# Gated-delta inverse: blocks of 16 solved on VectorE by way of DRAM, with small moves around it

## The chip, the cores and the metric

One core of one Trainium2 chip runs the whole program. The metric is the device time of one execution in microseconds (us); the kernel before was run three times, and its median is what a change is held against. The trace is of one more execution, taken by the profiler.

## The reference

The input is one sequence of 256 tokens, 1024 wide, in float32. Two "first" layers and then two "second" layers run over it. A first layer is a norm, a product with `w_in`, four mixers on the slices of its result, a product with `w_out`, a residual, and a gated feed-forward network (FFN). The four mixers are a (HGRN2) and b (gated linear attention), both chunkwise linear attention; c (latent attention with a softmax); and d, the gated delta rule. The second layers have other mixers and are not touched, but for a norm. What mixer d computes for each chunk of 64 tokens and each head is:

```
m   = strict_lower(kb @ kc^T * lmask)              # 64 x 64
sol = triangular_solve(m + eye, [v * b, kb * exp(b)])
u, w = split(sol)
v_new = u - w @ state
o     = (q * exp(b)) @ state + a_qk @ v_new
state = exp(b_last) * state + (k * exp(b_last - b))^T @ v_new
```

The linear mixers a and b need, for each chunk, the lower triangle of `attn[i, j] = sum_d q[i, d] k[j, d] exp(b[i, d] - b[j, d])`.

## The kernel before

The 256 tokens are two tiles t of 128 (all 128 partitions). Weights come from DRAM in units of up to 512 KB (`raw`, three buffers), whose DMAs SyncE (SP) issues in program order. Each is split into a rounded high part (`wh`, ScalarE, L300) and a remainder (`wl`, VectorE or GpSimd, L303), and each product is three passes on TensorE (L329 to L331, or L375 and L376). PSUM has eight banks in four pairs, acc, pc, pd and pa. Mixers a and b take their scratch from pa, c from pc, d from pd (`pt()`), and `acc()` hands out acc and pa in turn.

The mixers are Python generators that emit instructions in pieces; `PLAN1` and `RUN1` say whose piece comes next (d's preparation, b's projections, d's inverse and output, a's projections, b's attention, c, a's attention). From what was emitted a list scheduler fixes the order of instructions on each engine before the program runs. An engine works strictly in that order, so an instruction that waits holds up all that stand behind it on its engine. Between layers `steps()` and `sum_sq()` run the residual and the norms, and `warm()` may put in bf16 matmuls whose result nobody reads.

Mixer d prepares, per tile, `MT` and `AT` (L1128, L1129): the triangular matrix transposed, four heads of 128x128, each with two chunks of 64 on its diagonal. Then (I + M) is inverted by doubling blocks. At a level w = 2, 4, 8 or 16, with the inverse `V` of the diagonal blocks of w known and `T` its transposed even blocks, TensorE multiplies `MT` with `T` (L1176, four heads a tile), VectorE masks the product into `X` (L1177), TensorE multiplies `X` with `V` (L1191), VectorE adds that to `V` (L1192), TensorE transposes `V` (L1197) and ScalarE copies the transpose into `T` (L1199). GpSimd clears `X` (L1174). Before the first level VectorE writes the blocks of 2 with masks (L1154, L1155). Levels 32 and 64 go by smaller pieces (L1168, L1184). With the inverse in hand come d's output steps for tile 0, the state, and tile 1 (L1205 to L1240), each closed by a norm over heads (`head_norm`, L601 to L608), transposes of its result (L415), and the hi and lo part of it (L417, L418) for the product with `w_out`.

The linear mixers a and b (`gla`) build the triangle the same way on scaled queries and keys (`gl_r`, `gl_e`, L733, L727; products L743, L751): the diagonal block comes from PSUM by a multiplication with the identity (L705, VectorE), the levels 64 by a ScalarE copy (L756), and 32 down to 1 by copies under a mask (L760, VectorE). Then L768 and L769 multiply with the values. Mixer c's product with `w_in` is 48 passes of 128x416 (L329 to L331), alternately into acc and pa.

Of the kernel before, what the change touches and what calls it, by code (L numbers as in the profile page):

```python
# [11 lines left out]
F = mybir.dt.float32  # L12
# [34 lines left out]
WARM = ((0, 0, 0), (0, 2, 0))  # L47
# [92 lines left out]
class K:  # L140
    def __init__(self, ctx, tc, a):
        self.tc, self.nc, self.a = tc, tc.nc, a
        e = ctx.enter_context
        self.cst = e(tc.tile_pool(name="cst", bufs=1))
        self.wp = e(tc.tile_pool(name="wp", bufs=1))
        self.xp = e(tc.tile_pool(name="xp", bufs=1))
        self.zp = e(tc.tile_pool(name="zp", bufs=1))
        self.sm = e(tc.tile_pool(name="sm", bufs=4))
        self.ps = e(tc.tile_pool(name="ps", bufs=1, space=PSUM))
        self.units, self.made, self.nexti, self.emitted = [], {}, 0, 0  # L150
# [12 lines left out]
        nc.vector.memset(self.mhalf, -0.5)  # L163

    def masks(self):
# [5 lines left out]
        nc.gpsimd.tensor_copy(self.cu, t)  # L171

# [250 lines left out]
    def sum_sq(self, a, b, psum=False):  # L423
# [5 lines left out]
        self.warm(sc, WARM[self.g == "a"][0 if psum else 2])  # L429
# [261 lines left out]
    def gla(self, nft, b, qm, k, v, finish, g):  # L691
# [8 lines left out]
        for t in range(2):  # L700
# [4 lines left out]
            nc.vector.tensor_tensor(A[t], p, self.ident[:, None, :].to_broadcast([128, 4, 128]), OP.mult)  # L705
# [3 lines left out]
        for lv, s in enumerate((128, 64) + LEVELS):  # L709
# [181 lines left out]
    def mixer_c(self, l, xT):  # L891
# [12 lines left out]
        pz = self.tm(xT, (("c", l), 2, 416))  # L904
# [93 lines left out]
    def mixer_d(self, l, xT):  # L998
# [3 lines left out]
        code = [self.z([128, 16], "b_code", "b") for _ in range(2)]  # L1002
# [38 lines left out]
        def prep(t):  # L1041
# [5 lines left out]
            nbeta = self.s(4, "d_nbeta")  # L1047
            nc.vector.tensor_scalar(nbeta, beta, -1.0, None, op0=OP.mult)
# [42 lines left out]
            nc.vector.tensor_tensor(kb, qk[:, 4:8], bc4(nbeta, 64), OP.mult)  # L1091
# [9 lines left out]
            kT = self.z([128, 2, 2, 128], "d_kT")  # L1101
            nc.gpsimd.memset(kT, 0.0)
# [11 lines left out]
            for par in range(2):  # L1114
                rr = slice(par * 64, par * 64 + 64)
                nc.scalar.activation(kT[rr, par], p2[rr, :2], AF.Copy)
            if t:
                o["qeT"] = self.z([128, 2, 128], "d_qeT")
                nc.scalar.activation(o["qeT"], p2[:, 2:], AF.Copy)
# [22 lines left out]
        for t in range(2):  # L1142
            T[t] = self.z([128, 4, 64], "d_T")
            V[t] = self.z([128, 4, 128], "d_V")
            nc.gpsimd.tensor_copy(part(T[t], 2), half(mb(self.ident), 2, 0))
            nc.gpsimd.tensor_copy(V[t], mb(self.ident))
        for t in range(2):
            MT = st[t]["MT"]
# [3 lines left out]
            at = lambda i, n: self.cu[:, i * 64:i * 64 + 64].rearrange("p (b s) -> p b s", s=n)[:, None].to_broadcast(  # L1152
                [128, 4, 64 // n, n])
            nc.vector.copy_predicated(part(T[t], 2), at(6, 2), half(p, 2, 0))  # L1154
            nc.vector.copy_predicated(half(V[t], 1, 1), at(5, 1), half(MT, 1, 1))  # L1155
        for lv in range(6):
            w = 2 << lv
            X = [None] * 2
            for t in range(2):
# [17 lines left out]
                nc.vector.tensor_tensor(half(X[t], w, 0), part(p, w), half(mb(ms[:, lv * 128:lv * 128 + 128]), w, 0), OP.mult)  # L1177
            for t in range(2):
                p = self.pt()[:, :256].rearrange("p (h i) -> p h i", h=4)
                if w >= 32:  # L1180
# [11 lines left out]
                nc.vector.tensor_tensor(v, v, part(p, w), OP.add)  # L1192
# [37 lines left out]
        nc.scalar.activation(wT[:64], pw, AF.Copy)  # L1230
# [7 lines left out]
        for h in range(4):  # L1238
            nc.tensor.matmul(po[:, h], st[1]["qeT"][:, h // 2], Sp[:, h], start=True, stop=False)
# [548 lines left out]
```

## Time and profile before

| | before |
|---|---|
| times of three runs, us | 1532.23, 1531.16, 1528.4 |
| median, us | 1531.16 |
| profiled execution: its own time, its span, us | 1537.6, 1535.9 |
| mean granted TensorE clock | 0.989 of full |
| busy, share of the span | TensorE 96%, VectorE 69%, ScalarE 55%, GpSimd 18% |
| bytes moved, rate | 233.99 MB, 152 GB/s |

Read it so: the span is what the profiler saw from the first to the last instruction of the profiled execution. PE is TensorE's matmuls, PEld its weight loads (they run beside matmuls), DVE is VectorE, ACT ScalarE, POOL GpSimd, SP SyncE. The clock is the part of full speed that the chip granted to TensorE. In rows of the timeline the first number is when an instruction, or a group of neighbours of one kind, began, the second its busy time. Since matmuls are pipelined, the records of a group overlap the next: what a group costs TensorE is read from start to start.

### The profile page before, as it was taken

The numbers are of one execution on the slowest core, as the hardware profiler recorded it, in microseconds if no ns is written. First come the engines' busy times: TensorE is split into PE (matmuls) and PEld (weight loads), VectorE is DVE, ScalarE is ACT, GpSimd is POOL, SyncE is SP. The second block draws the span as 40 slices with busy tenths as digits, with TensorE's granted clock in tenths as the row PEclk, the third lists the DMA queues.
The fourth block names the chain that finished last, engine by engine and source line by source line (L and its number), as shares of the span: only waits on it lengthen the run. The fifth ranks groups of instructions, "written<-read, shape, count | busy, mean of one in ns | idle before, by whom it ended". The sixth has DMA issues, their size and how long they took to land.

```text
span 1535.9 us, 23550 instructions
## 1 busy us (share of the span) xinstructions
PE 1481.3 (96%) x8731; PEld 1287.0 (84%) x8739; DVE 1062.3 (69%) x1891; ACT 837.2 (55%) x1520; POOL 281.8 (18%) x375
## 2 busy tenths in 40 slices
PE   7999999999998999999999999999998999999998
PEld 7988888888897987888978887888877888888886
DVE  6897577667789756777766866566657695666655
ACT  5735456556574534655545665544554675544453
POOL 1544210000254322000042122000024231100010
PEclk9999999999999999999999999999999999999999
DMA  7422146666452214666646334566653533465663
GB/s 238 150 84 100 52 140 184 190 190 213 135 161 78 93 42 134 183 192 187 206 131 184 110 112 124 187 191 191 211 186 111 163 121 108 133 192 187 190 202 108
DMA packets 156418, 233.99 MB, mean 152 GB/s; under 512 B 11700, under 2 KB 118158, under 8 KB 156302
## 3 DMA queue, kind: packets, MB, share of 16 engines
q1 hardware_dynamic: 156302, 232.48, 49.0%
q8 instruction: 69, 1.13, 0.3%
q14 instruction: 47, 0.39, 0.1%
HBM read 231.40 MB, written 1.05 MB: 151 GB/s over the span
## 4 chain that ended last, share of the span: by engine, by line
PE 79%; DVE 10%; ACT 4%; POOL 2%; DMA 2%; issue 2%; SPq 0%; ACTq 0%; DVEq 0%; POOLq 0%
PE pa L375 8%; PE pd L375 7%; PE acc L329 7%; PE acc L331 7%; PE acc L330 7%; PE pc L329 5%; PE pc L331 5%; PE pc L330 5%; PE pd L376 4%; PE pa L376 4%; PE pa L329 2%; PE pa L331 2%; PE pa L330 2%; DVE wl L303 2%; DVE gl_r L733 1%
## 5 line engine op out<-in xcount | busy, mean ns | idle before, releaser
L303 DVE TENSOR_TENSOR wl<-raw,wh 128x1024 fp32r<-128x1024 f32 (+4 forms) x424 | 487.1, 1157 | 310.2 <-ACT wh L300 308.6
L300 ACT ACTIVATE wh<-raw 128x1024 fp32r<-128x1024 f32 (+4 forms) x420 | 433.1, 1035 | 368.9 <-PE pc L331 92.1
L303 POOL TENSOR_TENSOR wl<-raw,wh 128x1024 fp32r<-128x1024 f32 (+1 forms) x26 | 61.2, 2358 | 641.8 <-ACT wh L300 611.2
L375 PE MATMUL pa<-xT,wh 128*128 128x512 f32 x392 | 145.9, 397 | 0.0
L375 PE MATMUL pd<-xT,wh 128*128 128x512 f32 x392 | 145.7, 397 | 0.0
L376 PE MATMUL pd<-xT,wl 128*128 128x256 f32 x392 | 110.2, 281 | 0.3 <-DVE wl L303 0.3
L376 PE MATMUL pa<-xT,wl 128*128 128x256 f32 x392 | 110.1, 281 | 0.0
L375 PEld LDWEIGHTS pd<-xT,wh 128*128 128x128 f32 x392 | 73.6, 188 | 16.8
L375 PEld LDWEIGHTS pa<-xT,wh 128*128 128x128 f32 x392 | 73.7, 188 | 12.3
L330 PE MATMUL acc<-wl,f_h 128*128 128x512 f32 x200 | 78.0, 390 | 0.0
L330 PE MATMUL pc<-wl,f_h 128*128 128x512 f32 x200 | 77.8, 389 | 0.0
L331 PE MATMUL pc<-wh,f_l 128*128 128x512 f32 x200 | 77.5, 389 | 0.0
L331 PE MATMUL acc<-wh,f_l 128*128 128x512 f32 x200 | 77.3, 391 | 0.0
L376 PEld LDWEIGHTS pd<-xT,wl 128*128 128x128 f32 x392 | 74.0, 189 | 3.6 <-DVE wl L303 0.5
L376 PEld LDWEIGHTS pa<-xT,wl 128*128 128x128 f32 x392 | 74.1, 189 | 3.6
L330 PE MATMUL acc<-wl,xT 128*128 128x512 f32 (+4 forms) x200 | 71.1, 357 | 1.6 <-DVE wl L303 1.6
L329 PE MATMUL acc<-wh,xT 128*128 128x512 f32 (+4 forms) x200 | 71.5, 361 | 1.2 <-ACT xT L510 0.8
L329 PE MATMUL pc<-wh,f_h 128*128 128x512 f32 x200 | 71.4, 390 | 0.0
L331 PE MATMUL acc<-wh,xT 128*128 128x512 f32 (+4 forms) x200 | 70.4, 354 | 0.6 <-DVE xT L512 0.6
L329 PE MATMUL acc<-wh,f_h 128*128 128x512 f32 x200 | 67.0, 391 | 0.0
L329 PE MATMUL acc<-wh,mT 128*128 128x512 f32 (+2 forms) x136 | 51.4, 387 | 1.6 <-ACT mT L510 1.4
L330 PE MATMUL acc<-wl,mT 128*128 128x512 f32 (+2 forms) x136 | 51.3, 378 | 0.0
(651 smaller groups left out, 3852.5 us busy)
## 6 DMA issues: line engine op xcount, KB each, us to landing
raw<-in_w_in_dram SPq DMA_DIRECT2D x84, 512.0 KB, 4.2
raw<-in_w_mlp_up_dram SPq DMA_DIRECT2D x64, 512.0 KB, 3.7
raw<-in_w_mlp_down_dram SPq DMA_DIRECT2D x64, 512.0 KB, 3.6
raw<-in_ffn_w_gate_dram SPq DMA_DIRECT2D x44, 512.0 KB, 3.6
raw<-in_ffn_w_up_dram SPq DMA_DIRECT2D x44, 512.0 KB, 3.9
raw<-in_ffn_w_down_dram SPq DMA_DIRECT2D x44, 512.0 KB, 3.6
raw<-in_w_out_dram SPq DMA_DIRECT2D x32, 512.0 KB, 3.6
raw<-in_w_ple_gate_dram SPq DMA_DIRECT2D x16, 512.0 KB, 4.4
```

What stands on the lines that cost most here:

```text
L300: nc.scalar.activation(h[:, p], raw[:, p], AF.Copy)
L303: e.tensor_tensor(l[:, p], raw[:, p], h[:, p].bitcast(F), OP.subtract)
L329: t.matmul(out, ah, bh, start=first, stop=False, skip_group_check=True)
L330: t.matmul(out, ah, bl, start=False, stop=False, skip_group_check=True)
L331: t.matmul(out, al, bh, start=False, stop=last, skip_group_check=True)
L375: t.matmul(out[f], h[:, k, c], xT.both[:, :, kk], start=kk == 0, stop=False, skip_group_check=True)
L376: t.matmul(out[f][:, 1], l[:, k, c], xT[0][:, kk], start=False, stop=kk == 7, skip_group_check=True)
L733: nc.vector.tensor_tensor(R[:, j].rearrange("p h (b s) -> p h b s", s=s), ev[:, ft[j], :, 1][:, None].to_broadcast([128, 2, 128 // s, s]), ...
```

## The change

Mixer d's levels 2, 4 and 8 are gone, and so are the masks that fed them. In their place the program does this: both tiles of `MT` go to a DRAM buffer `scr`, whose pitch of 129 rows per head makes the blocks of 16 on the diagonal addressable by one stride; one DMA brings the 64 blocks of 16x16 back, one block to a partition (`Z`, 1024 pieces of 64 bytes); VectorE inverts all of them by forward substitution (seven pairs of a product and a reduction over up to 98 elements, then two pairs over 512); `Y` goes in pieces of 64 bytes to a second DRAM buffer `scv`, which was zeroed at the program's start; and two DMAs (256 KB each) bring the block-diagonal `V` of both tiles. TensorE transposes `V`, ScalarE copies it into `T`, and the old loop goes on from level 16. The sign of M is turned, so copies get `scale=-1` and one addition becomes a subtraction.

Around it: `gla` takes its diagonal by a ScalarE copy and a GpSimd `affine_select`, and level 32 by four small ScalarE copies for each tile in place of one masked copy; mixer c's product goes into the bank pair acc alone; `kT` in d's preparation is one dense copy, and its matmul reads 64 partitions; `code` lies in another pool; the constants shrink; and the norm before three of the layers gets four warm matmuls (128x512, bf16) for tile 0. At the start four more DMAs of 132 KB zero `scv`.

```diff
-WARM = ((0, 0, 0), (0, 2, 0))
+WARM = ((0, 0, 0, 4), (0, 2, 0, 0))
...
-        self.warm(sc, WARM[self.g == "a"][0 if psum else 2])
+        self.warm(sc, WARM[self.g == "a"][0 if psum else 2 + (self.near > 0 and self.kinds[self.near] in PEORD)])
...
+        zero = self.z([128, 258], "zero", "d")
+        nc.gpsimd.memset(zero, 0.0)
+        for i in range(4):
+            nc.sync.dma_start(self.at(self.scv, i * 128 * 258, [[258, 128], [1, 258]]), zero)
...
-            nc.vector.tensor_tensor(A[t], p, self.ident[:, None, :].to_broadcast([128, 4, 128]), OP.mult)
+            nc.scalar.activation(A[t], p, AF.Copy)
+            nc.gpsimd.affine_select(out=A[t], in_=A[t], pattern=[[0, 4], [1, 128]], compare_op=OP.is_ge, fill=0.0,
+                                    base=0, channel_multiplier=-1)
...
+                if s == 32:
+                    for r in (0, 64):
+                        nc.scalar.activation(A[t][r:r + 32, :, r + 32:r + 64], pv[r:r + 32, :, r // 2:r // 2 + 32], AF.Copy)
+                    continue
...
-        pz = self.tm(xT, (("c", l), 2, 416))
+        pz = self.tm(xT, (("c", l), 2, 416), outs=self.first_banks("acc"))
...
-            kT = self.z([128, 2, 2, 128], "d_kT")
-            nc.gpsimd.memset(kT, 0.0)
...
+            kT = self.z([128, 4, 128], "d_kT")
+            nc.scalar.activation(kT[:, :4 if t else 2], p2[:, :4 if t else 2], AF.Copy)
...
-                    nc.tensor.matmul(p[:, f], kT[:, par, f], qkT[:, f], start=True, stop=True)
+                    nc.tensor.matmul(p[:, f], kT[rr, f], qkT[rr, f], start=True, stop=True)
...
+        for t in range(2):
+            nc.sync.dma_start(dense(self.scr, t), st[t]["MT"])
+        Z, Y = self.z([64, 256], "d_Z"), self.z([64, 256], "d_Y")
+        nc.sync.dma_start(Z.rearrange("p (j r) -> p j r", r=16), blocks(self.scr))
+        nc.gpsimd.tensor_copy(Y, self.cb[:64, 512:768])
+        tmp, U = self.z([64, 512], "d_tmp"), self.z([64, 64], "d_U")
+        for r in range(1, 8):
+            p = tmp[:, :2 * r * r].rearrange("p (a c j) -> p a c j", a=2, c=r)
+            nc.vector.tensor_tensor(p, view(Z, r, [[136, 2], [0, r], [16, r]]), view(Y, 0, [[136, 2], [16, r], [1, r]]), OP.mult)
+            nc.vector.tensor_reduce(view(Y, r, [[136, 2], [16, r]]), p, AX.X, OP.add, negate=True)
...
+        nc.sync.dma_start(blocks(self.scv), Y.rearrange("p (c r) -> p c r", r=16))
...
+            nc.sync.dma_start(V[t], dense(self.scv, t))
             p = four()
             for h in range(4):
-                nc.tensor.transpose(p[:, h], MT[:, h], self.ident)
...
-            nc.vector.copy_predicated(part(T[t], 2), at(6, 2), half(p, 2, 0))
-            nc.vector.copy_predicated(half(V[t], 1, 1), at(5, 1), half(MT, 1, 1))
-        for lv in range(6):
+                nc.tensor.transpose(p[:, h], V[t][:, h], self.ident)
+            T[t] = self.z([128, 4, 64], "d_T")
+            nc.scalar.activation(part(T[t], 16), half(p, 16, 0), AF.Copy)
+        for lv in range(3, 6):
```

The line numbers of the kernel of the change are higher by 16 to 31 than those of the same code before: L329 to L331 are L345 to L347 there, L303 L319, L415 L431, L733 L752, L751 L770, L760 L783, L1176 L1207, L1240 L1271. The order of the instructions moves at three places. First TensorE in the first layer, before, where level 8 ends and mixer c's product (128x416) begins:

```order
L1176 MATMUL pd<-d_T,d_MT 128x64 x4
L1191 MATMUL pd<-d_V,d_X 128x64 x8
L1197 MATMUL pd<-cf,d_V 128x128 x8
L415 MATMUL pa<-cf,hn_o 128x128 x2
L329 MATMUL pa<-wh,xT 128x416
L330 MATMUL pa<-wl,xT 128x416
```

and in the kernel of the change the place where the inverse comes back to TensorE, behind the end of b's attention (L791, L792, L431) and ahead of a's (L720) and c's (L951):

```order
L792 MATMUL pa<-a_v,gl_a 128x64
L1184 MATMUL pd<-cf,d_V 128x128 x8
L1207 MATMUL pd<-d_T,d_MT 128x64 x8
L431 MATMUL pa<-cf,hn_o 128x128 x2
L720 MATMUL pa<-gl_q,a_k 128x256 x2
L951 MATMUL pc<-cf,c_cn 128x128 x2
L1222 MATMUL pd<-d_V,d_X 128x64 x4
```

Before, 30 passes of 128x416 (mixer c's product) came after the small levels had ended, 22 of them behind the start of level 16; now 26 passes stand right behind the last `MT` matmul (L1144), ahead of b's products L770, and the 8 transposes L1184, which need `V`, stand ahead of all that follows.

Second, VectorE in the first layer of the kernel of the change, from the last `MT` (L1145) to the first step of the substitution (L1164):

```order
L1145 TENSOR_TENSOR d_MT<-pd,d_L 128x2x128
L1146 TENSOR_TENSOR d_AT<-pd,d_L 128x2x128
L319 TENSOR_TENSOR wl<-raw,wh 128x1024
L746 TENSOR_TENSOR gl_e<-b_b 128x32x4
L752 TENSOR_TENSOR gl_r<-gl_e,gl_q 128x256 x6
L319 TENSOR_TENSOR wl<-raw,wh 128x1024
L1164 TENSOR_TENSOR d_tmp<-d_Z,d_Y 64x2
L1165 TENSOR_REDUCE d_Y<-d_tmp 64x2
```

From L1164 to the last reduction (L1170) VectorE has 18 instructions of the substitution and 26 others between them: 8 `gl_r` (L752), 2 `gl_e` (L746), 10 masked copies (L783), 3 `wl` (L319) and 3 of b's head norm (L619, L622, L624).

Third, SP's queue in the second of the first layers of the kernel of the change, from the first tile of `MT` on its way to DRAM to `V`:

```order
L1157 DMA scr<-d_MT 128x4x128
L306 DMA raw<-in_w_out_dram 128x1024
L1159 DMA d_Z<-scr 64x16x16
...
L306 DMA raw<-in_w_out_dram 128x1024
L1171 DMA scv<-d_Y 64x16x16
L306 DMA raw<-in_ffn_w_gate_dram 128x4x256
L1181 DMA d_V<-scv 128x4x128 x2
```

In the first layer the same queue has `scv<-d_Y` and `d_V` next to each other; here a unit of `w_gate` stands between them. At the end of the mixers TensorE's order has also moved: before, c's last transposes and products (L655, L666) and two passes of the product with `w_out` stood between d's last L1240 and the transposes L415 of its head norm; now L431 (the transposes) follows L1271 (the old L1240) at once, and c's pieces stand ahead of it.

## Rows read from the trace of the kernel before

**Rows 1.** The page, busy time by engine and the chain that ended last.
```profile
PE 1481.3 (96%) x8731; PEld 1287.0 (84%) x8739; DVE 1062.3 (69%) x1891; ACT 837.2 (55%) x1520; POOL 281.8 (18%) x375
...
PE 79%; DVE 10%; ACT 4%; POOL 2%; DMA 2%; issue 2%; SPq 0%; ACTq 0%; DVEq 0%; POOLq 0%
```

**Rows 2.** Windows, first layer: window, length, busy by engine, granted clock, DMA.
```profile
84.00:97.00 13.00, 11.31 (x54) 9.38 (x52) 13.00 (x28) 4.70 (x11) 8.03 (x14) 1.00 0.37 115
...
97.00:126.10 29.10, 28.44 (x217) 27.52 (x217) 20.59 (x54) 6.37 (x17) 9.13 (x20) 0.88 0.10 30
126.10:182.00 55.90, 54.24 (x446) 47.27 (x444) 40.16 (x91) 30.12 (x87) 20.22 (x38) 1.00 0.25 86
```

**Rows 3.** Lines of TensorE over the run: busy, mean ns | idle before.
```profile
L1176 PE MATMUL pd<-d_T,d_MT 128*128 128x64 f32 x128 | 18.1, 289 | 0.0
L1191 PE MATMUL pd<-d_V,d_X 128*128 128x64 f32 x128 | 16.8, 281 | 0.0
L1197 PE MATMUL pd<-cf,d_V 128*128 128x128 f32 x80 | 11.6, 276 | 0.3
```

**Rows 4.** Timeline of TensorE, both first layers: start, busy, instruction.
```profile
105.03 1.00 PE L1176 MATMUL pd<-d_T,d_MT 128*128 128x64 f32 x8
105.87 0.39 PE L1191 MATMUL pd<-d_V,d_X 128*128 128x64 f32 x2
...
126.14 1.00 PE L1176 MATMUL pd<-d_T,d_MT 128*128 128x64 f32 x8
...
127.41 0.35 PE L330 MATMUL pa<-wl,xT 128*128 128x416 f32 x1
127.60 0.35 PE L331 MATMUL pa<-wh,xT 128*128 128x416 f32 x1
...
514.56 0.44 PE L1176 MATMUL pd<-d_T,d_MT 128*128 128x64 f32 x3
```

**Rows 5.** Timeline of VectorE, both first layers.
```profile
96.61 0.45 DVE L1128 TENSOR_TENSOR d_MT<-pd,d_L 128x256 f32<-128x256 f32 x1
...
98.49 2.31 DVE L733 TENSOR_TENSOR gl_r<-gl_e,gl_q 128x256 f32<-128x256 f32 x6
...
109.25 0.76 DVE L760 COPY_PREDICATED gl_a<-cu,pa 128x256 f32<-128x256 uint8 x2
...
481.24 0.45 DVE L1128 TENSOR_TENSOR d_MT<-pd,d_L 128x256 f32<-128x256 f32 x1
```

**Rows 6.** Lines of VectorE by shape, 57 to 165 us.
```profile
L303 DVE TENSOR_TENSOR wl<-raw,wh 128x1024 fp32r<-128x1024 f32 x14 | 18.2, 1303 | 1.7 <-ACT wh L300 1.7
...
L1084 DVE TENSOR_REDUCE d_ssq<-d_sq 128x8 f32<-128x512 f32 x2 | 1.4, 679 | 0.1
...
L629 DVE TENSOR_SCALAR sm_nb<-sm_mx 128x2 f32<-128x2 f32 x3 | 0.5, 158 | 0.0
```

**Rows 7.** DMA queues (packets, MB, share of 16 engines), and issues with us to landing.
```profile
q1 hardware_dynamic: 156302, 232.48, 49.0%
...
raw<-in_ffn_w_gate_dram SPq DMA_DIRECT2D x44, 512.0 KB, 3.6
...
out_dram<-x SPq DMA_DIRECT2D x4, 256.0 KB, 2.0
...
2_lk<-in_lambda_k_dram SPq DMA_DIRECT2D x4, 16.0 KB, 3.0
```

**Rows 8.** DMA queue in the window 555 to 575 us.
```profile
q1 hardware_dynamic: 820, 0.10, 2.8%
```

**Rows 9.** Timeline of TensorE at the end of the first layer's mixers.
```profile
176.47 0.39 PE L1240 MATMUL pd<-d_vn,d_AT 128*128 128x64 f32 x2
...
182.01 0.50 PE L329 MATMUL pc<-wh,mT 128*128 128x512 f32 x1 [0.31 <-ACT mT L417]
```

**Rows 10.** Windows just behind two of the layers' boundaries, columns as in rows 2.
```profile
787.00:791.00 4.00, 4.00 (x15) 2.94 (x14) 4.00 (x8) 2.77 (x5) 1.53 (x2) 0.57 0.01 2
...
1159.00:1166.50 7.50, 6.50 (x20) 5.24 (x21) 5.33 (x10) 2.64 (x5) 2.73 (x3) 0.54 0.00 0
```

More of the change, by code (lines that the diff above doesn't have):

```diff
@@ L68, in host_constants @@
     c["after"] = (i > j)
-    ms = []
-    for s in (2, 4, 8, 16, 32, 64):
-        ms.append((i // (2 * s) == j // (2 * s)) & (i // s % 2 == 1) & (j // s % 2 == 0))
+    m16 = (i // 32 == j // 32) & (i // 16 % 2 == 1) & (j // 16 % 2 == 0)
+    eye16 = np.tile(np.eye(16).reshape(1, 256), (128, 1))
     c["causal"] = np.where(j <= i, 0.0, NEG)
@@ L89, in host_constants @@
         lm.append(P[:, None] // s == 2 * (jj // s)[None])
-    jj = np.arange(64)[None]
-    lm.append((P[:, None] == jj // 2 * 4 + 1) & (jj % 2 == 0))
-    cm = np.concatenate([np.eye(128), np.where(j <= i, 0.0, NEG), np.where(j > i, 0.0, NEG)] + ms, 1)
+    cm = np.concatenate([np.eye(128), np.where(j <= i, 0.0, NEG), np.where(j > i, 0.0, NEG), m16, eye16], 1)
     inv = np.concatenate([10000.0 ** (-np.arange(32) / 32.0), 10000.0 ** (-np.arange(16) / 16.0)])
@@ L149, in __init__ @@
         self.ps = e(tc.tile_pool(name="ps", bufs=1, space=PSUM))
+        self.dr = e(tc.tile_pool(name="dr", bufs=1, space=bass.MemoryType.DRAM))
+        self.scr = self.dr.tile([8 * 129, 128], F, name="scr")
+        self.scv = self.dr.tile([8 * 129, 128], F, name="scv")
         self.units, self.made, self.nexti, self.emitted = [], {}, 0, 0
@@ L171, in masks, with at, view @@
         nc.gpsimd.tensor_copy(self.cu, t)
+        zero = self.z([128, 258], "zero", "d")
+        nc.gpsimd.memset(zero, 0.0)
+        for i in range(4):
+            nc.sync.dma_start(self.at(self.scv, i * 128 * 258, [[258, 128], [1, 258]]), zero)
+    @staticmethod
+    def at(t, offset, dims):
+        t = t[:]
+        return bass.AP(tensor=t.tensor, offset=t.offset + offset, ap=dims)
+    @staticmethod
+    def view(t, offset, dims):
+        return bass.AP(tensor=t.tensor, offset=t.offset + offset, ap=[list(t.ap[0])] + dims)
     def c(self, name):
@@ L1001, in mixer_d @@
         pz = self.tm(xT, (("dz", l), 2, 280))
-        code = [self.z([128, 16], "b_code", "b") for _ in range(2)]
+        code = [self.xp.tile([128, 16], F, name=f"code{t}", bufs=1) for t in range(2)]
         for t in range(2):
@@ L1090, in prep @@
             kb = self.z([128, 4, 64], "d_kb")
-            nc.vector.tensor_tensor(kb, qk[:, 4:8], bc4(nbeta, 64), OP.mult)
+            nc.vector.tensor_tensor(kb, qk[:, 4:8], bc4(beta, 64), OP.mult)
             if t == 0:
@@ L1113, in prep @@
             nc.scalar.activation(qkT, p1, AF.Copy)
[L1114 to L1119, printed above, removed]
+            kT = self.z([128, 4, 128], "d_kT")
+            nc.scalar.activation(kT[:, :4 if t else 2], p2[:, :4 if t else 2], AF.Copy)
+            o["qeT"] = kT
             yield
@@ L1133, in mixer_d @@
         self.g = "d"
+        dense = lambda m, t: self.at(m, t * 4 * 129 * 128, [[128, 128], [129 * 128, 4], [1, 128]])
+        blocks = lambda m: self.at(m, 0, [[16 * 129, 64], [128, 16], [1, 16]])
+        view = self.view
+        for t in range(2):
[8 more added lines that the diff above has]
+            nc.vector.tensor_reduce(view(Y, r, [[136, 2], [16, r]]), p, AX.X, OP.add, negate=True)
+        p = tmp.rearrange("p (c r j) -> p c r j", c=8, r=8)
+        nc.vector.tensor_tensor(p, view(Y, 0, [[16, 8], [0, 8], [1, 8]]), view(Z, 8, [[0, 8], [1, 8], [16, 8]]), OP.mult)
+        nc.vector.tensor_reduce(U.rearrange("p (c i) -> p c i", c=8), p, AX.X, OP.add)
+        nc.vector.tensor_tensor(p, view(U, 0, [[8, 8], [0, 8], [1, 8]]), view(Y, 136, [[0, 8], [1, 8], [16, 8]]), OP.mult)
+        nc.vector.tensor_reduce(view(Y, 8, [[16, 8], [1, 8]]), p, AX.X, OP.add, negate=True)
+        nc.sync.dma_start(blocks(self.scv), Y.rearrange("p (c r) -> p c r", r=16))
         T, V = [None] * 2, [None] * 2
-        ms = self.cb[:, 384:]
         half = lambda x, w, odd: x.rearrange("p h (b two s) -> p h b two s", two=2, s=w)[:, :, :, odd]
@@ L1176, in mixer_d @@
                     nc.tensor.matmul(p[:, h], st[t]["MT"][:, h], T[t][:, h], start=True, stop=True)
-                nc.vector.tensor_tensor(half(X[t], w, 0), part(p, w), half(mb(ms[:, lv * 128:lv * 128 + 128]), w, 0), OP.mult)
+                nc.vector.tensor_tensor(half(X[t], w, 0), part(p, w), half(mb(self.cb[:, 384:512]), w, 0), OP.mult)
             for t in range(2):
@@ L1191, in mixer_d @@
                     nc.tensor.matmul(p[:, h], X[t][:, h], v[:, h], start=True, stop=True)
-                nc.vector.tensor_tensor(v, v, part(p, w), OP.add)
+                nc.vector.tensor_tensor(v, v, part(p, w), OP.subtract)
             for t in range(2):
@@ L1229, in mixer_d @@
         nc.gpsimd.memset(wT[64:], 0.0)
-        nc.scalar.activation(wT[:64], pw, AF.Copy)
+        nc.scalar.activation(wT[:64], pw, AF.Copy, scale=-1.0)
         pu = self.pt()[:, :256].rearrange("p (h d) -> p h d", h=4)
@@ L1238, in mixer_d @@
         for h in range(4):
-            nc.tensor.matmul(po[:, h], st[1]["qeT"][:, h // 2], Sp[:, h], start=True, stop=False)
+            nc.tensor.matmul(po[:, h], st[1]["qeT"][:, 2 + h // 2], Sp[:, h], start=True, stop=False)
             nc.tensor.matmul(po[:, h], st[1]["AT"][:, h], v1[:, h], start=False, stop=True)
```

12 lines of the change are left out of this document (2 added, 10 removed).

## The prediction

> **What bounds the kernel now.** I read the page first. TensorE is busy 96% of the span, and of the chain of waits that ended last 79% is TensorE's and 10% VectorE's [rows 1]. So a saving counts where it takes TensorE's time, and a wait counts where TensorE has nothing else to do. The windows show where that is not plain [rows 2]. In the first layer, from 84 to 97 us, VectorE is busy all 13.00 us and TensorE 11.31: d's preparation hangs on VectorE. From 97 to 126.1, the time of the levels 2, 4 and 8 beside b's attention, TensorE is busy 28.44 of 29.1 us at a granted clock of 0.88, from 126.1 to 182 it is busy 54.24 of 55.9 us at full clock. So before the change the small levels hide no idle time; their work costs TensorE what it takes.
>
> **What goes.** The lines L1176 and L1191 run at the levels 2, 4, 8 and 16, L1197 at these and at 32. Of the 128, 128 and 80 records over both layers [rows 3] the three removed levels thus own 3/4, 3/4 and 3/5: 96, 96 and 48. They waited for next to nothing. From start to start, eight records of L1176 take 105.87 - 105.03 = 0.84 us [rows 4], 0.105 each. 240 of them make 25.2 us over two layers, 12.6 each. If nothing took the place, this would be the gain.
>
> **What comes.** A trip: `MT` to DRAM, 64 blocks back, substitution on VectorE, `Y` to DRAM, `V` back. TensorE's order puts the transposes of `V` ahead of a's attention and c's preparation, so all of that waits for the trip. I time it from t0, the start of the last `MT` on VectorE: 96.61 in the first layer and 481.24 in the second [rows 5]. In the new order I read t0 at 96.2 (a diagonal L705 and a mask less ahead of it) and 481.9 (a `wl` more ahead).
>
> - `MT` ends at t0 + 0.45 [rows 5]. A write to DRAM of 256 KB lands in 2.0 us and a small read in 3.0 [rows 7]; with 0.2 us for each issue, `Z` is there at t0 + 5.9 if its 1024 pieces of 64 bytes cost little. VectorE first has `AT`, two `wl` and six `gl_r` and is there at about t0 + 6. I take 6.2.
> - The price of the pieces. Each of 16 DMA queues gets 64 of them. In the window of small packets, 820 packets (0.10 MB, 122 bytes each) took 2.8% of 16 engines for 20 us, 10.9 ns each [rows 8]; over the whole run a packet of 1.5 KB took 77 ns [rows 7]. So 64 pieces cost 0.7 to 4.9 us. I take 0.7, inside the small read's 3.0, because the cheap row is the one with the nearest size.
> - The Trainium skill, "DMA: Bandwidth & Descriptors", section "Specifications", speaks against the change: line rate needs transfers of 512 bytes or more, below that the engine reads, modifies and writes. By that rule the pieces would cost more than their bytes say, the sum would move toward the upper end of the first rival below, and no run here has shown it for writes of 64 bytes.
> - VectorE from the first step to the last. Own work: 14 small instructions at 0.17 (0.158 is the smallest row) make 2.4, four over 512 elements at 0.68 make 2.7 [rows 6]. In between stand 8 `gl_r` at 2.31 / 6 = 0.39, 10 masked copies at 0.38 [rows 5], 3 `wl` at 1.3 [rows 6], 3 head-norm steps at 0.45 (the 128x256 row in [rows 5]) and 2 `gl_e` at half a `gl_r`: 3.1 + 3.8 + 3.9 + 1.35 + 0.4 = 12.5. Together 17.6, so `Y` is ready at t0 + 23.8.
> - `Y` out 0.2 + 2.0, `V` in 0.2 + 3.3 (256 KB, between the 3.0 of 16 KB and the 3.6 of 512 KB [rows 7]): t0 + 29.5. Four transposes (0.42) and a copy: level 16 starts at t0 + 30.5. In the second layer a 512 KB unit stands on SP's queue ahead of `V`: 0 to 3.6 more [rows 7], I take the half, 1.8.
>
> Level 16 thus begins at 126.7 where it began at 126.14, and at 514.2 where it began at 514.56 [rows 4]: **+0.6 and -0.4, +0.2** in all. So the removed 25.2 us do not come off: TensorE gets a hole instead. In it TensorE has at most the 28.44 of [rows 2] less 12.6, plus the passes moved in, some 20 us for 30.
>
> **What the hole is filled with.** 22 passes of mixer c's product stood behind the start of level 16 and now stand ahead of it. A pass takes 127.60 - 127.41 = 0.19 us [rows 4], so the tail, which was 97% busy [rows 2], gets 4.2 us shorter for each layer: **-8.4**. At worst the tail is a chain that does not shorten: 0.
>
> **The end of the mixers.** Before, c's pieces and two passes of the next product filled the time of d's last head norm, from the last L1240 at 176.47 to the next product at 182.01 [rows 9]. Now only four transposes stand there. The chain of that norm is 5.5 us long, of which the pieces filled some 3.7; they run earlier now, into holes if the tail has any (1.66 us of idle in the tail before [rows 2]). 0.3 to 3.7 per layer, I take 1.8: **+3.6**.
>
> **Warm matmuls.** Behind two boundaries the mean granted clock is 0.57 over 4.0 us and 0.54 over 7.5 us [rows 10], so nearly all at the lower of its two levels (1.2 of 2.4 GHz); that lost 0.43 x 4.0 = 1.7 and 0.46 x 7.5 = 3.4 us, 5.1 in all. Four passes in the idle time ahead may hold the clock up, cost nothing there, and they stand at a third boundary too, for which I count nothing. Ends 0 and -5.1, I take the half: **-2.5**.
>
> **The start.** Zeroing `scv` puts 528 KB on SP's queue, the constants lose 130. At 512 KB in 3.6 us [rows 7] that is up to 2.8 us; behind it stand gains, not the first weights. **+0.5**.
>
> **Costed at nothing.** ScalarE's copies (a diagonal and four pieces of level 32 per tile) and GpSimd's select replace work of VectorE; ScalarE was busy 6.37 of 29.1 and 30.12 of 55.9 us, GpSimd 9.13 and 20.22 [rows 2], which covers some 2 us more on ScalarE per layer. If that cover were gone, the masked copies would come later and level 16 with them, one for one. VectorE's savings in 126.1 to 182 save nothing, since it was busy 40.16 of 55.9 there. Bank pair acc for c takes pa from nobody.
>
> **Sum:** +0.2 - 8.4 + 3.6 - 2.5 + 0.5 = -6.6. The profiled execution had 1537.6 us around a span of 1535.9 and lies 0.4% above the median of 1531.16; against the median the forecast is **1524.6 us**. A measurement of this kernel tells 0.3%, 4.6 us, from no change, so this is faster by a little more than that. With the ends of its own terms (tail, end of mixers, warm) the case spans 1518 to 1528.
>
> **Rivals.**
> 1. *The pieces are dear.* Each of 64 pieces on a queue costs 77 ns instead of 10.9 [rows 7, 8]: 4.2 us more for `Z` and 4.2 for `Y` in each layer. `V` then lands at about t0 + 38, and as TensorE's transposes stand ahead of a's and c's work each of these microseconds counts: +16.8, **1541.4**, slower. It decides from 5.6 us more per layer, where the sum passes 1535.8. For it speaks that no transfer of before has pieces so small both ways; against it the 10.9 ns row. Half of it would give 1533. Chance 0.24.
> 2. *The hole is given back.* After a hole TensorE runs at half clock, as behind the boundaries [rows 10], and loses 1.7 to 3.4 us per layer behind the wait; the end of the mixers is exposed by 3.7 instead of 1.8. That is +5.3 to +10.6 on the forecast: **1530 to 1535**, no change. For it speaks that both clock rows follow idle time; against it that the steps behind the wait (transpose, copy, matmul, mask) leave TensorE waiting anyhow. Chance 0.27.
> 3. *The trip hides.* VectorE's interleaved work could be scheduled tighter than I add it, and TensorE never wait: then the 25.2 come off, with warm and start 1531.2 - 25.2 - 2.0 = **1504**. Against it stands that the sum of the trip has no spare: it would have to be 10 us shorter. Chance 0.09.
> The forecast itself has 0.40.
>
> **How the numbers follow.** Faster by over 0.3%: the forecast without its upper edge (0.38) and rival 3 (0.09), 0.47. Within: rival 2 and that edge, 0.29. Slower: rival 1, 0.24. The range 1510 to 1541 leaves out rival 3 and the upper half of rival 1, 0.2 together.
>
> **What would show it.** In the profile after: TensorE idle ahead of L1184 by 5 us or more, released by the DMA of `V`; `Z` landing within 3 to 4 us of its issue; level 16 beginning within 2 us of 126.7; between level 16 and the end of the mixers some 4 us less for TensorE per layer; a gap ahead of L431 at the end; a clock over 0.8 behind the boundaries of [rows 10]. The prediction is wrong if `V` lands more than 5 us later than t0 + 30, if the time from level 16 to the next product with `w_out` is not shorter, or if TensorE does not wait at L1184 at all.

## The result and the profile after

The change is slower: 1551.68 us against 1531.7 (medians of four runs each), with a ratio on record of 1.0126 (not quite the ratio of these two medians), 95% interval 1.0104 to 1.0147. I had forecast 1524.6 and a range up to 1541. The profiled execution took 1549.0 us, 2.7 below its median; that of before lay 5.9 above its own, so between the two traces only 11.4 us show. The mean granted clock of TensorE, recorded for every execution, says why: the traced execution of before ran at 0.989, while 74 others on record, on four chips, ran at 0.991 to 0.997, and 0.004 of 1536 us are 6 us. The four of the change ran at 0.976 to 0.980. One further execution of before, at 2076.77 us and a clock of 0.653, is left out as slow. The page of the changed kernel, its busy line, the granted clock in 40 slices and the chain, against [rows 1]:

```profile
PE 1471.1 (95%) x8502; PEld 1265.4 (82%) x8511; DVE 1050.6 (68%) x1875; ACT 842.3 (54%) x1530; POOL 286.4 (19%) x362
...
PEclk9997999999999699999999999999999999999999
...
PE 77%; DVE 10%; DMA 4%; ACT 4%; POOL 2%; issue 2%; SPq 0%; DVEq 0%; ACTq 0%; POOLq 0%
```

TensorE's work did fall (1481.3 to 1471.1 us), and DMA took 4% of the chain instead of 2%. The two low digits of the clock stand where the inverses of the two first layers are. The windows of the first layer (columns as in [rows 2]), from d's preparation to the next product with `w_out`:

```profile
84.00:97.00 13.00, 13.00 (x58) 9.99 (x58) 12.94 (x27) 5.92 (x12) 7.09 (x10) 1.00 0.47 134
97.00:105.00 8.00, 8.00 (x51) 7.37 (x49) 6.38 (x16) 5.17 (x10) 3.01 (x5) 1.00 0.74 200
105.00:130.60 25.60, 14.13 (x68) 12.66 (x67) 18.45 (x42) 6.13 (x14) 9.07 (x12) 0.60 0.47 145
130.60:188.80 58.20, 53.60 (x426) 46.49 (x424) 32.77 (x84) 26.46 (x87) 20.47 (x41) 0.94 0.08 22
```

Until 105 us TensorE is busy all the time, where it was busy 11.31 of 13 us from 84 to 97 before. Then comes the hole: 14.13 busy of 25.6 us, at a granted clock of 0.60, so for the most part at 1.2 GHz. And the tail behind level 16, which I expected 4.2 us shorter, took 58.2 us where it took 55.9. The timeline of VectorE, from the last `MT` to the substitution's last reduction, against [rows 5]:

```profile
96.27 0.41 DVE L1145 TENSOR_TENSOR d_MT<-pd,d_L 128x256 f32<-128x256 f32 x1
...
103.83 0.15 DVE L1164 TENSOR_TENSOR d_tmp<-d_Z,d_Y 64x2 f32<-64x2 f32 x1 [0.67 <-DMA d_Z<-scr]
...
117.59 0.42 DVE L619 TENSOR_REDUCE hn_ssq<-hn_sq 128x4 f32<-128x256 f32 x1 [0.93 <-ACT hn_sq L617]
117.93 1.01 DVE L1167 TENSOR_TENSOR d_tmp<-d_Y,d_Z 64x512 f32<-64x512 f32 x1
119.03 1.23 DVE L319 TENSOR_TENSOR wl<-raw,wh 128x1024 fp32r<-128x1024 f32 x1
...
122.45 0.41 DVE L624 TENSOR_TENSOR hn_o<-hn_y,a_g 128x256 f32<-128x256 f32 x1
122.78 0.67 DVE L1170 TENSOR_REDUCE d_Y<-d_tmp 64x64 f32<-64x512 f32 x1
```

and of TensorE, from the last pass of c's product through the hole to the end of the mixers, against [rows 4] and [rows 9]:

```profile
101.80 0.35 PE L347 MATMUL acc<-wh,xT 128*128 128x416 f32 x1
...
115.17 1.97 PE L792 MATMUL pa<-a_v,gl_a 128*128 128x64 f32 x8 [0.81 <-DVE d_Y L1165]
123.00 0.66 PE L431 MATMUL pa<-cf,hn_o 128*128 128x128 f32 x2 [5.87 <-DVE hn_o L624]
...
128.76 2.09 PE L1184 MATMUL pd<-cf,d_V 128*128 128x128 f32 x8 [1.79 <-DMA d_V<-scv]
130.65 3.52 PE L1207 MATMUL pd<-d_T,d_MT 128*128 128x64 f32 x16
...
187.98 0.41 PE L431 MATMUL pd<-cf,hn_o 128*128 128x128 f32 x2 [3.08 <-DVE hn_o L624]
188.86 0.80 PE L345 MATMUL pc<-wh,mT 128*128 128x512 f32 x1 [0.47 <-ACT mT L433]
```

All of c's passes are over at 102 us, before the hole begins. The longest wait in the hole, 5.87 us, is not for `V` but for b's head norm: between its steps L619 and L624 VectorE's queue holds steps of the substitution and a `wl`. The wait for `V` itself is 1.79 us. Level 16 starts at 130.65, and its 16 records take 3.31 us from start to start, where the same 16 cost 1.68 at full clock [rows 4]. At the end TensorE waits 3.08 and 0.47 us for d's head norm. The clock is low behind both waits (columns as in [rows 2]): behind level 16 with TensorE busy throughout, and behind the end of the mixers, where 3.4 us at 1.2 GHz lose another 1.7.

```profile
130.00:140.00 10.00, 10.00 (x54) 9.46 (x54) 5.49 (x20) 4.10 (x20) 3.89 (x11) 0.64 0.11 36
188.40:191.80 3.40, 2.94 (x7) 2.36 (x8) 0.42 (x1) 0.38 (x1) 0.00 (x0) 0.50 0.02 5
```

The DMAs of the trip (issue to landing, as in [rows 7]) of 256 KB took 3.9 and 4.2 us, the two of 64 KB in 64-byte pieces 2.7 and 2.5:

```profile
scr<-d_MT SPq DMA_DIRECT2D x4, 256.0 KB, 4.2
d_V<-scv SPq DMA_DIRECT2D x4, 256.0 KB, 3.9
...
d_Z<-scr SPq DMA_DIRECT2D x2, 64.0 KB, 2.7
scv<-d_Y SPq DMA_DIRECT2D x2, 64.0 KB, 2.5
```

### The profile page after: what moved, and what is told of

Its sections match the earlier page's. It is cut to its first block, busy times and chain, and to the rows that moved or that the text cites. A ratio compares the mean times of both kernels' runs of the same rounds, so it can differ in the third digit from the quotient of the medians.

```text
span 1547.3 us, 23071 instructions
## 1 busy us (share of the span) xinstructions
PE 1471.1 (95%) x8502; PEld 1265.4 (82%) x8511; DVE 1050.6 (68%) x1875; ACT 842.3 (54%) x1530; POOL 286.4 (19%) x362
## 4 chain that ended last, share of the span: by engine, by line
PE 77%; DVE 10%; DMA 4%; ACT 4%; POOL 2%; issue 2%; SPq 0%; DVEq 0%; ACTq 0%; POOLq 0%
PE pa L391 7%; PE pd L391 7%; PE acc L347 7%; PE acc L345 7%; PE acc L346 7%; PE pc L345 5%; PE pc L346 5%; PE pc L347 5%; PE pd L392 4%; PE pa L392 4%; PE pa L345 2%; PE pa L346 2%; PE pa L347 2%; DVE wl L319 2%; ACT wh L316 1%
## 5 line engine op out<-in xcount | busy, mean ns | idle before, releaser
L319 DVE TENSOR_TENSOR wl<-raw,wh 128x1024 fp32r<-128x1024 f32 (+4 forms) x424 | 484.4, 1150 | 315.2 <-ACT wh L316 313.6
L319 POOL TENSOR_TENSOR wl<-raw,wh 128x1024 fp32r<-128x1024 f32 (+1 forms) x26 | 60.6, 2335 | 641.1 <-ACT wh L316 641.1
L347 PE MATMUL acc<-wh,f_l 128*128 128x512 f32 x200 | 78.4, 397 | 0.0
L347 PE MATMUL pc<-wh,f_l 128*128 128x512 f32 x200 | 78.2, 393 | 0.0
L345 PE MATMUL acc<-wh,xT 128*128 128x512 f32 (+4 forms) x216 | 76.6, 358 | 1.0 <-ACT xT L526 0.8
L347 PE MATMUL acc<-wh,xT 128*128 128x512 f32 (+4 forms) x216 | 75.9, 353 | 0.8 <-DVE xT L528 0.8
L346 PE MATMUL acc<-wl,xT 128*128 128x512 f32 (+4 forms) x216 | 75.7, 352 | 0.0
L345 PE MATMUL pc<-wh,f_h 128*128 128x512 f32 x200 | 72.3, 394 | 0.0
L345 PE MATMUL acc<-wh,f_h 128*128 128x512 f32 x200 | 67.5, 393 | 0.0
L345 PE MATMUL acc<-wh,mT 128*128 128x512 f32 (+2 forms) x136 | 49.4, 372 | 1.6 <-ACT mT L526 1.1
L347 PE MATMUL acc<-wh,mT 128*128 128x512 f32 (+2 forms) x136 | 50.1, 373 | 0.6 <-DVE mT L528 0.6
```

The costliest lines, as they stand in the source:

```text
L319: e.tensor_tensor(l[:, p], raw[:, p], h[:, p].bitcast(F), OP.subtract)
L345: t.matmul(out, ah, bh, start=first, stop=False, skip_group_check=True)
L346: t.matmul(out, ah, bl, start=False, stop=False, skip_group_check=True)
L347: t.matmul(out, al, bh, start=False, stop=last, skip_group_check=True)
```

## The experiments

The theories: **C**, TensorE has nothing to do in the hole, its clock falls there, and the time is lost through the hole and behind it; **L**, only the trip's length counts; **O**, the other edits cost the time. From e5 on, **F**: c's passes of 128x416 are the work with which TensorE bridges the levels, and in the bank pair acc they are spent before they are needed. Ratios are to the kernel before on the same chip.

**e1, the change with unread matmuls in the hole.**

```diff
+    def fill(self, src, n, tag):
+        p = self.bank(tag)[:, :256]
+        for _ in range(n):
+            self.nc.tensor.matmul(p, self.ident[:src.shape[0]], src, start=True, stop=True)
...
         nc.scalar.activation(sq, src, AF.Square)
+        if m == 1 and not t:
+            self.fill(sq.rearrange("p a b -> p (a b)"), 12, "pc")
...
         nc.sync.dma_start(blocks(self.scv), Y.rearrange("p (c r) -> p c r", r=16))
+        self.fill(Y, 5, "pd")
```

> The change, with matmuls that nobody reads put on TensorE in the hole ahead of V's transposes: 12 of 128x256 behind the first half of b's output product, 5 behind the last step of the substitution. The trip itself is left as it is. Theory C (the clock): half of the loss is TensorE running at the lower clock through the hole and for some 9 us behind it, about 4 us per layer; with the clock held the transposes take 0.11 us instead of 0.23 each, the granted clock behind V is over 0.9, and the time falls by 5 to 8 us, to about 1.008 to 1.009 of before. Theory L (only the length of the trip counts): the clock does not matter, since the steps behind V wait for each other; no change within 2 us, 1.0126. Theory O (the other edits cost the time): no change either.

Measured: 1.0049 (1.0032 to 1.0066), 12 us faster than the change, more than theory C asked. Its timeline of TensorE and the window of its tail:

```profile
118.16 8.20 PE L471 MATMUL pc<-hn_sq,cf 128*128 128x256 f32 x24 [0.47 <-ACT hn_sq L623]
...
130.64 1.04 PE L1193 MATMUL pd<-cf,d_V 128*128 128x128 f32 x8
131.72 2.00 PE L1216 MATMUL pd<-d_T,d_MT 128*128 128x64 f32 x16
...
183.45 0.50 PE L345 MATMUL pc<-wh,mT 128*128 128x512 f32 x1 [0.47 <-ACT mT L433]
```

```profile
131.70:183.40 51.70, 49.37 (x422) 43.12 (x422) 31.49 (x84) 26.40 (x87) 22.18 (x44) 1.00 0.07 22
```

Level 16 starts 1.1 us later than in the change, and yet the tail ends 5.4 us earlier: 51.7 us at a clock of 1.00 instead of 58.2 at 0.94. Theory L's claim that the clock does not matter falls, since V came no sooner. The traced execution, 1533.87 us at a mean clock of 0.992, is the fastest of the twelve (median 1540.45), so a usual one gains less than this trace shows.

**e10, the control for e1**: the same with `fill(..., 1, "pc")` and `fill(Y, 1, "pd")`.

> e1 with one unread matmul at either place in place of 12 and 5: the control for e1, since the added instructions also move the order of some pieces behind level 16. Theory C: with one matmul the clock falls as in the change, 1.010 to 1.013. If e1's gain came from the order that moved and not from the clock: 1.005 to 1.008.

Measured: 1.0112 (1.0093 to 1.0131). Its windows show the change's clock again:

```profile
120.00:130.00 10.00, 5.35 (x22) 4.46 (x22) 6.74 (x13) 2.59 (x9) 4.24 (x8) 0.50 0.38 106
130.00:140.00 10.00, 10.00 (x56) 9.32 (x57) 5.22 (x16) 3.11 (x13) 4.51 (x13) 0.65 0.18 59
```

and its timeline of TensorE:

```profile
131.70 3.52 PE L1216 MATMUL pd<-d_T,d_MT 128*128 128x64 f32 x16
...
188.65 0.80 PE L345 MATMUL pc<-wh,mT 128*128 128x512 f32 x1 [0.47 <-ACT mT L433]
```

So of e1's gain 0.6 per cent, some 9.7 us, come with the number of unread matmuls. The order behind level 16 is not quite the same in the two, so a part of that is order. In the first layer the traces allow a split, since level 16 begins at the same time in both (131.72 in e1, 131.70 here): the next product with `w_out` begins 5.2 us later here. From 131 to 140 us the clock is 0.66 here and 1.00 in e1, 3.1 us; at the end of the mixers TensorE waits 3.08 us for `hn_o` here and 1.35 in e1, where other work stands in that place, 1.7 us that I put down to order.

**e2, all edits but the trip.** The kernel before with every hunk of the diff that does not belong to the inverse by way of DRAM; two of them:

```diff
-WARM = ((0, 0, 0), (0, 2, 0))
+WARM = ((0, 0, 0, 4), (0, 2, 0, 0))
...
-        pz = self.tm(xT, (("c", l), 2, 416))
+        pz = self.tm(xT, (("c", l), 2, 416), outs=self.first_banks("acc"))
```

> The kernel before with all edits except the inverse: warm matmuls, the diagonal and level 32 by ScalarE and GpSimd, c's product in the bank pair acc, the dense kT, code in another pool; the levels 2, 4 and 8 stay on TensorE. Theories C and L: the whole loss is in the trip by way of DRAM, so this is 2 to 8 us faster than before (0.995 to 0.999), from the warm matmuls and VectorE's relief. Theory O: it is slower than before by over 8 us (above 1.005), because TensorE's order at the end of the mixers moves with c's bank pair.

Measured: 1.0091 (1.0069 to 1.0114), against C and L, for O. Without any trip the time is lost too.

**e9, one line of it alone**: the `pz` line above, on the kernel before.

> The kernel before with one line of the change: c's product in the bank pair acc. Theory F (the passes are TensorE's filler and are spent early, at the same cost whether the inverse goes by TensorE or by DRAM): as slow as e2, 1.006 to 1.011, with a hole and the lower clock between the levels 8 and 16. If the bank pair hurts only together with the other edits: 0.998 to 1.002.

Measured: 1.0087 (1.006 to 1.0115). One line, which adds and removes no work, costs 13 us. Its timelines of TensorE and of VectorE, and windows:

```profile
99.88 0.35 PE L331 MATMUL acc<-wh,xT 128*128 128x416 f32 x1
...
107.16 1.10 PE L1176 MATMUL pd<-d_T,d_MT 128*128 128x64 f32 x8 [2.65 <-DVE d_T L1154]
...
136.37 3.56 PE L1176 MATMUL pd<-d_T,d_MT 128*128 128x64 f32 x16
```

```profile
102.79 2.75 DVE L303 TENSOR_TENSOR wl<-raw,wh 128x1024 fp32r<-128x1024 f32 x2
...
106.67 0.43 DVE L1154 COPY_PREDICATED d_T<-cu,pd 128x256 f32<-128x256 uint8 x1
```

```profile
105.00:115.00 10.00, 7.84 (x56) 7.84 (x57) 9.39 (x26) 2.16 (x4) 2.38 (x4) 0.83 0.46 145
...
120.00:130.00 10.00, 8.49 (x56) 7.88 (x55) 4.89 (x11) 2.20 (x5) 2.36 (x6) 0.77 0.34 107
130.00:140.00 10.00, 10.00 (x49) 9.92 (x48) 2.32 (x9) 2.85 (x14) 3.86 (x12) 0.50 0.00 0
```

c's passes are spent at 100 us; the levels then wait for VectorE and ScalarE with nothing between them, the clock falls, and level 16 begins at 136.37 where it began at 126.14 [rows 4]. Theory F's number holds, but the trace shows more than passes that are spent early: with them the splits of the weights (`wl`) move forward on VectorE. Between the last `MT` and level 16 VectorE has five of them, 6.4 us, where it had none before, and two stand ahead of the mask L1154 for which TensorE waits 2.65 us. What the missing cover costs and what the splits cost was not separated.

**e3 and e5, the square.** e3 is the change with the `pz` line taken back; e5 is e2 with the `pz` line taken back.

```diff
-        pz = self.tm(xT, (("c", l), 2, 416), outs=self.first_banks("acc"))
+        pz = self.tm(xT, (("c", l), 2, 416))
```

> The change, but c's product alternates between acc and pa as before. Then 26 passes of 128x416 fall behind V again, the hole is emptier and the tail longer by up to 5 us per layer. Theories C and L: V lands when it did, so 5 to 10 us slower than the change (1.016 to 1.019). Theory O (the bank pair is what costs): faster than the change by 5 us or more (below 1.0095).

> The kernel before with the edits around the inverse but neither the trip nor c's product in the bank pair acc: warm matmuls, the diagonal and level 32 by ScalarE and GpSimd, dense kT, code in another pool. With e2 (the same and c in acc) it closes a square of four: trip or not, acc or alternate. Theory F (c's 128x416 passes are the work with which TensorE holds its clock between the levels; in acc they are all spent at once): 0.996 to 1.001, so that e2's 1.0091 is the bank pair's; and the trip alone, e3 over this one, costs 0.7 to 1.2 per cent. Theory G (ScalarE's and GpSimd's new copies make the linear mixers late): 1.005 or more.

Measured: e3 1.0084 (1.0062 to 1.0107), e5 0.9996 (0.9986 to 1.0007). e3 missed what C and L said, and came out just inside O's bound.

| | c's product alternates acc and pa | in acc |
|---|---|---|
| levels 2, 4, 8 on TensorE | 0.9996 (e5) | 1.0091 (e2), 1.0087 (e9) |
| the trip by way of DRAM | 1.0084 (e3) | 1.0126 (the change) |

Each of the two edits costs some 0.9 per cent alone, and both together 1.26, not 1.8; I read that as both spending the same cover, which is not shown by itself. In e5 the other edits (warm matmuls, ScalarE, GpSimd, kT, code) come to nothing in sum, so theory G, which put the loss on these, falls. Its executions ran at a mean clock of 0.997 to 1.000, above before's, and yet in the same time; which of the edits takes back what the clock gives no run shows. The same stretch in e3 and then in e5:

```profile
105.00:115.00 10.00, 4.25 (x32) 3.76 (x32) 9.57 (x30) 0.38 (x1) 1.92 (x5) 0.84 0.28 85
...
120.00:130.00 10.00, 7.72 (x34) 7.39 (x34) 2.55 (x6) 1.54 (x4) 1.21 (x2) 0.50 0.17 52
```

```profile
105.00:115.00 10.00, 9.93 (x90) 9.65 (x89) 6.37 (x15) 1.92 (x5) 2.05 (x5) 1.00 0.29 85
...
120.00:130.00 10.00, 9.97 (x71) 9.55 (x71) 6.29 (x11) 5.01 (x9) 2.26 (x6) 1.00 0.21 67
```

The levels 2, 4 and 8 themselves were cover: with them and c's passes in between, TensorE stays busy and at full clock. In e3 V does not land when it did in the change, as the expectation said, but 6 us earlier: VectorE has no `wl` between the last `MT` (97.45) and the last reduction, where the change has five from 97.92 on. Both rows are from e3:

```profile
116.21 0.67 DVE L1170 TENSOR_REDUCE d_Y<-d_tmp 64x64 f32<-64x512 f32 x1
...
124.44 3.52 PE L1207 MATMUL pd<-d_T,d_MT 128*128 128x64 f32 x16
```

**e11, e3 with unread matmuls** (12 and 4, where e1 had 12 and 5).

> e3 (the trip, c's product in alternate banks, so that 26 of its passes fill the tail) with unread matmuls in the hole, 12 and 4. Theory C: 5 to 8 us faster than e3 (1.003 to 1.005). Below 1.000 it would be the first version with the trip that beats the kernel before; I give that 1 in 5.

Measured: 1.003 (1.0016 to 1.0045), as C said. The unread matmuls give back 0.54 per cent of e3's 0.84, and the mean clock is nearly before's again (0.990 to 0.995, e3 0.980 to 0.984), so the rest does not show in the clock. A control like e10 was not run here, so order may have a part in it.

**e7, the trip made longer**: the write of `Y` stands twice.

```diff
         nc.sync.dma_start(blocks(self.scv), Y.rearrange("p (c r) -> p c r", r=16))
+        nc.sync.dma_start(blocks(self.scv), Y.rearrange("p (c r) -> p c r", r=16))
```

> The change with the write of Y to DRAM issued twice, the same bytes to the same place, so that V's read waits for the second: the trip is about 2.5 us longer in each layer and nothing else differs. If the length of the trip sets the time, 4 to 6 us slower than the change (1.0155 to 1.0165). If the trip has spare time behind b's last products, under 2 us.

Measured: 1.0164 (1.0146 to 1.0183), 0.38 per cent or 5.8 us over the change for one more write of 2.5 us in each layer; the two intervals touch. TensorE's wait for V grows from 1.79 to 5.58 us, at half clock for the work around it:

```profile
133.94 1.33 PE L1185 MATMUL pd<-cf,d_V 128*128 128x128 f32 x5 [5.58 <-DMA d_V<-scv]
```

So nothing hides the end of the trip, and by the ratios its length counts about one for one (theory L's half that holds). The traces are less even: from c's first pass to the next product with `w_out` the first layer grew by 3.1 us, the second by 0.3.

**e4, the substitution first**: b's masked copies and its levels 8 and below are queued behind the last reduction.

```diff
+    def behind(self, on):
+        return self.tc.issue_after(self.sub.ins) if on and self.g == GB[0] and self.inb else nullcontext()
...
+                with self.behind(lv >= 4):
...
+                with self.behind(True):
+                    nc.vector.copy_predicated(A[t].rearrange("p h (b two s) -> p h b two s", two=2, s=s)[:, :, :, 1],
...
+        self.sub = nc.vector.tensor_reduce(view(Y, 8, [[16, 8], [1, 8]]), p, AX.X, OP.add, negate=True)
```

> The change, with b's masked copies and the steps of its levels 8 and below queued on VectorE behind the last reduction of the substitution, so that nearly only wl splits stand between its steps. Y is then ready some 10 us earlier per layer, and TensorE's own order moves with it. Theory L: the time falls by 10 to 20 us (1.000 to 1.006), level 16 begins near 120 in the first layer instead of 130.7. Theory C alone: the hole moves rather than shrinks, 3 to 8 us (1.007 to 1.0105). Theory O: no change.

Measured: 1.0051 (1.0035 to 1.0066), inside theory L's range at its weak end: the shorter trip, with the order that moves along with it, gives back 0.75 per cent. Level 16 begins at 124.03, 6.6 us earlier than in the change, not near 120.

**e8, e4 with unread matmuls** on `Z` (12) and `Y` (8), and **e12**, e4's order on e3, with 4 on `Y`.

> The change with e4's order (b's copies behind the substitution) and unread matmuls on Z (12 of 128x256) and on Y (8) in TensorE's hole. Theory C: the clock is held over a hole that is also shorter, 6 to 10 us faster than e4 (0.998 to 1.001), the first chance to reach the kernel before. If the tail behind the hole is bound by its own chain, as e4's later start of the FFN hints (w_out's product began 9.5 us earlier, the FFN 3.8 us later), it stays at 1.003 to 1.005.

> The trip with c's product in alternate banks, b's copies behind the substitution as in e4, and 4 unread matmuls on Y: the two helps that do not rest on unread matmuls, put together. Theory F and C: c's passes fill the levels behind V, the hole ahead of V is shorter than in e3 and the clock falls for a shorter time: 0.999 to 1.004, better than e4's 1.0051. If b's delayed work and the chain behind it set the end of the mixers, as in e4's layer 0: 1.004 to 1.008.

Measured: e8 1.0109 (1.0082 to 1.0136), a miss: slower than e4 by 0.58 per cent. V's transposes began at 123.25 instead of e4's 120.55, behind the matmuls on `Y`, and b's late products queued behind them; I did not separate these two, so the cause is open. e12 1.0029 (1.0015 to 1.0044): as good as e11 with 4 unread matmuls for 16.

**e6, the change without the warm matmuls.**

```diff
-WARM = ((0, 0, 0, 4), (0, 2, 0, 0))
+WARM = ((0, 0, 0), (0, 2, 0))
```

> The change without the four warm matmuls ahead of three layers. If they hold the clock up behind the boundaries, as I forecast, this is 2 to 5 us slower than the change (1.014 to 1.016), with granted clocks under 0.7 at two boundaries. If they cost what they give, it is within 1.5 us of the change.

Measured: 1.014 (1.0125 to 1.0154), 0.14 per cent or 2.1 us over the change, inside both intervals and so not resolved. The clock behind the boundary, in the change and then in e6, is what I forecast:

```profile
799.50:803.50 4.00, 3.63 (x19) 2.50 (x18) 4.00 (x8) 2.87 (x5) 1.95 (x2) 1.00 0.01 4
```

```profile
801.50:806.50 5.00, 4.64 (x19) 3.89 (x20) 5.00 (x9) 2.75 (x5) 1.57 (x2) 0.69 0.01 3
```

No version with the trip reached the kernel before; e5 equals it.

## Why the prediction was wrong, step by step

Two steps of the sum failed: the 22 passes at -8.4, and the clock behind the wait, which the sum had at nothing.

- **What goes, and that it turns into a hole**: right. TensorE lost the work and waited. But the sign that I named, 5 us or more of waiting for `V` ahead of L1184, did not come: 1.79 us. The longest wait, 5.87 us, was for b's head norm, whose steps share VectorE with the substitution; I had not listed it.
- **The trip's parts**: nearly right in sum, each a little off. In the first layer, from t0 (96.27, forecast 96.2): first step at +7.6 for 6.2, since the write of 256 KB took 4.2 us and not the 2.0 of [rows 7]; the substitution to 123.45, 19.6 for 17.6, partly because a product over 512 elements took 1.0 us and not 0.68 [rows 6]; `Y` out and `V` in 5.3 for 5.7; transposes and copy 1.9 for 1.0, at half clock. Level 16 began at 130.65, not 126.7: 4 us. The 0.2 us for an issue came from no row; the issues of the trip took 0.4 to 0.7 us on SP's queue.
- **The price of the pieces**: right, and rival 1 is refuted in its mechanism. `Z` landed in 2.7 us and `Y` in 2.5, less than the 3.0 of a 16 KB read [rows 7]. The time came out on rival 1's side, but not by its way. By the Trainium skill ("DMA: Bandwidth & Descriptors", "Specifications") transfers under 512 bytes do not reach line rate. The trace does not contradict it: 64 KB in 2.7 us are some 24 GB/s, and the program's mean is 153. It shows only that 1024 such pieces need not land later than 16 KB.
- **"The hole is filled with 22 passes, -8.4"**: this step failed, and it has the largest part of the error. The change and e3 differ in this edit alone, and with it the time is 0.42 per cent, 6.4 us, longer (their intervals touch), not 8.4 shorter: 14.8 of the 26 us between the forecast of -6.6 and the measured 1.26 per cent, +19.3. A part of it is the clock's, below. The passes did leave the tail: in the first layer it took 62.3 us in e3 (124.44 to 186.76) and 58.2 in the change. But level 16 begins at 130.65 and not at 124.44, and with the passes five splits of weights, 6.1 us on VectorE, moved forward, ahead of the substitution and between its steps. I had these splits in the sum of the trip and did not charge them to this edit, which I otherwise put at nothing ("takes pa from nobody"). Nor did I ask where the passes had stood as cover: e9 shows that without any trip the same line costs 0.87 per cent.
- **The clock**: put at nothing in the sum, this is the second step that failed. Rival 2 had the mechanism, at 1.7 to 3.4 us a layer behind the wait. (By its own terms its lower end is +7.2, not +5.3.) In the first layer the tail ran at 0.94 of 58.2 us, 3.5 us lost, and 1.7 more just behind it. e10 and e1 put the gain of unread matmuls at about 9.7 us in all, e3 and e11 at 8.3, order included. My argument that the steps behind the wait leave TensorE waiting anyhow was wrong: from 130 to 140 us it was busy all 10.00 us, at 0.64.
- **The end of the mixers**: right in kind, undersized. 3.08 + 0.47 us of waiting, near the upper end of my 0.3 to 3.7; I took 1.8. Tail as forecast, 55.9 - 4.2 + 1.8 = 53.5; with 3.5 for the clock and 1.75 more of waiting 58.7; measured 58.2.
- **Second layer**: in the traces the stretch from c's first pass to the first pass behind the product with `w_out` grew by only 1.8 us (125.2 to 127.0) where the first layer's grew by 7.1 (117.0 to 124.1). But before's traced execution had lost clock there itself, 0.66 from 550 to 560 us, and it is the one with the lowest clock on record. In e5, as fast as before by the ratio, this stretch took 120.1 us. So the usual loss in the second layer is probably larger than 1.8 us, and the 8.6 us between the traces' difference and the medians' agree with the clocks: 5.9 us for before, 2.7 for the change, whose trace has the highest clock of its four (0.980).
- **Warm matmuls, start**: the clock was held as forecast; the worth is 2.1 us by the ratios, not resolved, for 2.5. The start moved 0.8 us earlier instead of 0.5 later.
- **The range of the case itself**: the ends that I gave for tail, end of mixers and warm matmuls add up to 1519 to 1539, not to 1518 to 1528. So the sum alone did not rule out a slower kernel.

What stays open: how much of the bank pair's cost is missing cover and how much the splits on VectorE; how the gain of the unread matmuls divides between clock and order outside the first layer of two traces; and what in e5 takes back its higher clock.

## What to carry to other kernels

Before taking work off the bottleneck engine, ask what it does while the chain that replaces that work runs: here the small levels cost TensorE some 25 us, counted from start to start, and were also the cover that kept it at full clock. An edit that only moves ready work earlier can cost as much as one that adds work: read from the order what stands between the dependent steps afterwards, and what the moved work brings with it on the other engines. And price a hole twice, for its length and for the lower clock in it and behind it.

## What the runs showed of the hardware that I had not expected

- DMAs of 1024 pieces of 64 bytes, 64 KB, landed in 2.5 us (to DRAM) and 2.7 us (from it), sooner than a dense write of 256 KB (4.2) or read (3.9) in the same program.
- With TensorE 14.13 of 25.6 us busy the granted clock was 0.60 on average and exactly 0.50 from 120 to 130 us; with 24 unread records from 118.16 on it was back at 1.00 by 130 (e1), and without them it was 0.64 from 130 to 140 although TensorE was busy all 10.00 us.
- A VectorE product of 64x512 through broadcast and strided views took 1.0 us where a reduction over as many elements took 0.67.
- Executions of one and the same program differ about as their mean granted clocks do: e1's range from 1533.87 us at 0.992 to 1544.43 at 0.985, 10.6 us where 0.007 of 1540 are 10.8.
